# A one-core decoder layer in fp32r: the order of instructions made with a timeline simulation in place of the plain machine model

## The chip, the cores and the metric

The kernel runs on one core of a Trainium2 chip. The metric is the device time of one launch in microseconds; lower is better. Engines are named as in the profile: PE is TensorE, DVE is VectorE, ACT is ScalarE, POOL is GpSimd and SP is SyncE, which issues most of the DMAs. L394 is line 394 of the kernel.

## The reference, cut to what matters

One layer on 1024 tokens of width 1024, all in float32: a norm, a token mixer of two parallel branches (RG-LRU and HGRN2), an output projection with a residual, a second norm, a squared-ReLU MLP with a residual, and a last norm.

```python
h = rms_norm(x, norm_mix)
xa, ga, q, f, v, g, m_a, m_b = split(h @ w_in)            # 8 projections of 1024 x 1024
y_a = rg_lru(conv4(xa), ...) * gelu(ga)                   # a scan over the tokens, channel by channel
o   = hgrn2_chunkwise(silu(q), k(f), log_f(f), v)         # 8 heads, chunks of 32 tokens, a 128x128 state per head
y_b = rms_norm(o, hg_norm) * silu(g)                      # norm over the 128 channels of a head
x   = x + (sigmoid(m_a) * y_a + sigmoid(m_b) * y_b) @ w_out
h   = rms_norm(x, norm_mlp)
x   = x + square(relu(h @ w_up)) @ w_down                 # 1024 -> 4096 -> 1024
out = rms_norm(x, norm_final)
```

## The kernel before

**Matrix products.** Each float32 operand is split into a high and a low fp32r part: ACT casts the high part (L76), DVE subtracts it from the source for the low part (L77). One product is then three matmuls of PE, high by high (L115), high by low (L116) and low by high (L117). Weights of the mixer come as tiles of 128 x 1024 (raw, L84), and each is split into wH and wL (`split_w`), two tiles ahead.

**Mixer.** The 1024 tokens are two chunks (c = 0, 1) of 512, and the 1024 channels are 4 pairs (p) of two 128-channel heads. A pair takes nine weight tiles' worth of projections in the order v, xa, q, f, rg, g, mb, ga, ma. From xa come the convolution (L301 to L311) and RG-LRU with its scan (L337 to L354); pr and pi are its two gate products. From q, f and v comes HGRN2: on each head the decay inside a chunk of tokens is built up in levels. PE multiplies small blocks of queries and keys into score banks (`sc1`, `sc2`, `sc8`, all L394, then `sc32` L479 and `sc64` L497); between the levels DVE multiplies queries and keys by further decays (L384, among them q, qb, kk and seg) and picks out the scores (L404, L438). Then, head after head (06 and 07, 16 and 17 are the two heads of the last pair), PE transposes the keys (`pk`, L525), ACT copies them (`kT`, L527), PE makes the state's increments (`pkv`, L531), DVE advances the state (`sn`, L545, L547), and PE makes the outputs (`po` of the pair, L538 and L541). ACT squares them for the norm of the head (`on`, L551) and copies them (L554), DVE adds the epsilon (`hssq`, L555), POOL raises to the power of -1/2 (`hrs`, L557) and DVE multiplies (on by hrs, L384). The gates follow (L565 to L596): PE transposes on (`poT`, L586), DVE multiplies it into `g2` (L587), and the sum `sma` (L595, L596) is split into y0H, y0L (chunk 0) or y1H, y1L, the operands of the output projection.

**Output projection and norms.** After the four pairs of chunk 0 comes `out_proj` (banks po000 to po013, weight tiles 68 to 75; the operand of the last pair meets wH71 and wH75), with the first norm of chunk 1 in between: the normed rows xn are transposed by PE (`xT_x`, L145) and split into hT. After chunk 1, the second output projection is mixed with the second norm: rows x2a and x2s, `norm_rows` (rstd_h, L137; xn_h, L139), transposes `xT_h` (L704), copies `braw` (L705), and sums and differences of quarters (`combos`, L666 to L669).

**MLP.** Both products are made with a seven-step scheme on quarters (X, Y and Z banks; `uX`, `uY`, `uZ` for up, `dX`, `dY`, `dZ` for down). Operands of the first are h2B11, h2T4 and the like, of the weights wA, ws1 to ws4. Up runs over 16 quads of 7 steps, and its squared results (b, then u, split once more) are kept in DRAM (L837, L897) but for the last two. Down runs over 8 blocks of two quads, in two halves of 7 steps each, and adds into acc (L963). `finish` (L924 to L934) is the last norm and the store.

**What sets the order.** The code above is the program's order; the order on every engine is made by the library's scheduler when the program is built. It places instructions one after another, taking among those that are ready by its view of when each engine is free and by priority. A few hints bind it: `keep_in_program_order` on the first norm of chunk 0, `tc.high_priority` of 400 around the weight splits, 300 around RG-LRU, 160 around the weights of one late quad. The pools limit it too: a tile is reused only after its last reader, with bufs tiles of a tag (4 of raw, 6 of w; of the PSUM banks 4 of pj for products, 2 of sc, and 2 of hg for the transposes and states). The engines then run their queues in that order, with semaphores for the dependences.

## Time and profile before

| | before |
|---|---|
| time, median of 3 runs (lowest to highest) | 1631.38 us (1631.27 to 1631.52) |
| span of the profiled execution, first to last instruction | 1628.7 us |
| mean granted clock of TensorE | 0.996 |
| busy: PE, DVE, ACT, POOL | 1584.9, 1212.7, 764.4, 65.8 us |
| moved by DMA | 246.51 MB, 151 GB/s |

The times are of whole launches; the profiled execution is known by its span, and the 2.7 us between it and the median lie outside the first and the last instruction. PE busy is the time in which at least one matmul is in the array; what it leaves of the span is idle time of PE. The stages follow each other in the trace: first norm to about 28 us, chunk 0 of the mixer to about 449, output projection to about 497, chunk 1 to about 927, its output projection and the second norm to about 1012, MLP up to about 1306, MLP down to about 1619, tail.

### The profile page before, as it was taken

Reading aid. Unit: us, or ns where it says so; the run is one execution under the profiler, and the core shown is the slowest. Engines: PE = TensorE matmul, PEld = TensorE weight load, DVE = VectorE, ACT = ScalarE, POOL = GpSimd, SP = SyncE. Lnnn points to the kernel's source line nnn. Section 1 sums busy time; section 2 is a strip of 40 time slices with the busy share of each in tenths; the row PEclk is TensorE's granted clock in tenths of the full one; section 3 lists DMA queues with packets and bytes.
Section 4 is the critical chain, followed back from the end, with each engine's and each line's share of the span. In section 5 each row is a group of like instructions: output and inputs, shape, how many; then the busy total and the mean of one; then the engine's idle time right before and its main releaser. Section 6 shows DMA issues by size and latency. Waiting matters only on the chain.

```text
span 1628.7 us, 23177 instructions
## 1 busy us (share of the span) xinstructions
PE 1584.9 (97%) x9240; PEld 1303.1 (80%) x9240; DVE 1212.7 (74%) x1751; ACT 764.4 (47%) x1186; POOL 65.8 (4%) x99
## 2 busy tenths in 40 slices
PE   7999999999999999999999997999999999999998
PEld 6788788788788788787787876888878878888886
DVE  5975956848764865848759688977777888888876
ACT  4643545435442544436434566766776731222113
POOL 0010100100100000100100100000000000000000
PEclk9999999999999999999999998999999999999999
DMA  6212212122243222222122352666656575666652
GB/s 237 91 66 91 91 66 103 66 91 91 80 167 136 86 78 90 80 78 101 69 91 91 117 207 104 250 246 250 235 233 248 222 269 228 251 244 251 254 203 104
DMA packets 57996, 246.51 MB, mean 151 GB/s; under 512 B 6688, under 2 KB 6816, under 8 KB 47136
## 3 DMA queue, kind: packets, MB, share of 16 engines
q1 hardware_dynamic: 56304, 239.27, 39.3%
q10 hardware_dynamic: 1584, 5.77, 1.0%
q8 instruction: 72, 1.18, 0.3%
q14 instruction: 36, 0.29, 0.1%
HBM read 185.24 MB, written 59.77 MB: 150 GB/s over the span
## 4 chain that ended last, share of the span: by engine, by line
PE 80%; DVE 16%; DMA 2%; issue 1%; ACT 1%; POOL 0%; DVEq 0%; POOLq 0%; SPq 0%; ACTq 0%
PE dX L115 3%; PE uX L115 3%; PE uX L117 3%; PE uX L116 3%; PE dX L116 3%; PE dX L117 3%; DVE wL L77 2%; PE pj_ga L117 2%; PE pj_ga L116 2%; PE pj_ga L115 2%; PE pj_f L117 2%; PE pv L115 2%; PE pv L117 2%; PE pv L116 2%; PE pj_ma L117 2%; PE pj_ma L116 2%
## 5 line engine op out<-in xcount | busy, mean ns | idle before, releaser
L77 DVE TENSOR_TENSOR wL<-raw,wH 128x1024 fp32r<-128x1024 f32 x160 | 194.3, 1214 | 150.0 <-ACT wH L76 145.8
L76 ACT CAST wH<-raw 128x1024 fp32r<-128x1024 f32 x160 | 167.9, 1050 | 168.1 <-issue 66.4
L963 DVE TENSOR_TENSOR acc<-acc,dX 128x512 f32<-128x512 f32 x128 | 85.2, 684 | 31.2 <-PE dX L117 30.1
L76 ACT CAST wA<-q 128x512 fp32r<-128x512 f32 x32 | 19.8, 621 | 129.6 <-PE dX L117 103.7
L963 DVE TENSOR_TENSOR acc<-acc,dY 128x512 f32<-128x512 f32 x64 | 43.6, 686 | 17.3 <-PE dY L117 15.7
L345 DVE RECIPROCAL rr<-rr 128x512 f32<-128x512 f32 x16 | 53.5, 3347 | 0.0
L823 ACT ACTIVATE b<-b 128x512 f32<-128x512 f32 x48 | 30.2, 631 | 38.6 <-DVE b L822 38.5
L115 PE MATMUL pv<-wH,hT0H 128*128 128x256 f32 x128 | 37.4, 292 | 0.0
L116 PE MATMUL pv<-wL,hT0H 128*128 128x256 f32 x128 | 37.0, 289 | 0.0
L117 PE MATMUL pv<-wH,hT0L 128*128 128x256 f32 x128 | 37.0, 289 | 0.0
L115 PE MATMUL pv<-wH,hT1H 128*128 128x256 f32 x128 | 36.5, 285 | 0.0
L117 PE MATMUL pv<-wH,hT1L 128*128 128x256 f32 x128 | 36.2, 283 | 0.0
L116 PE MATMUL pv<-wL,hT1H 128*128 128x256 f32 x128 | 36.2, 283 | 0.0
L311 DVE SCALAR_TENSOR_TENSOR xc<-xp,pvt,xc 128x512 f32<-128x512 f32 x48 | 33.1, 746 | 0.0
L551 ACT ACTIVATE on<-po 128x128 f32<-128x128 f32 x64 | 17.0, 278 | 33.5 <-PE po L541 33.2
L570 ACT ACTIVATE smb<-pj_mb 128x512 f32<-128x512 f32 x16 | 9.6, 598 | 45.3 <-PE pj_mb L117 45.2
L824 ACT ACTIVATE b<-b 128x512 f32<-128x512 f32 x48 | 30.1, 630 | 1.1
L77 DVE TENSOR_TENSOR wA<-q,wA 128x512 fp32r<-128x512 f32 x32 | 22.0, 687 | 9.9 <-ACT wA L76 9.7
L444 POOL TENSOR_SCALAR seg<-seg 128x128 f32<-128x128 f32 (+1 forms) x16 | 14.5, 905 | 361.1 <-DVE seg L384 361.1
L565 ACT ACTIVATE g<-pj_g 128x512 f32<-128x512 f32 x16 | 9.6, 600 | 37.2 <-PE pj_g L117 37.2
L384 DVE TENSOR_TENSOR seg<-seg 128x128 f32<-128x128 f32 (+2 forms) x96 | 26.7, 307 | 0.2
L117 PE MATMUL pj_ga<-hT1H,wL 128*128 128x512 f32 x64 | 26.5, 414 | 0.0
(1854 smaller groups left out, 5261.5 us busy)
## 6 DMA issues: line engine op xcount, KB each, us to landing
raw<-wts_in SPq DMA_DIRECT2D x160, 512.0 KB, 3.4
q<-mlp_in SPq DMA_DIRECT2D x64, 512.0 KB, 3.9
x<-x_in SPq DMA_DIRECT2D x8, 512.0 KB, 6.1
acc<-x ACTq DMA_DIRECT2D x8, 512.0 KB, 6.1
y_out<-acc SPq DMA_DIRECT2D x16, 256.0 KB, 2.1
xs<-x_in SPq DMA_DIRECT2D x8, 256.0 KB, 3.5
x<-xs SPq DMA_DIRECT2D x8, 256.0 KB, 2.3
x2s<-x_in SPq DMA_DIRECT2D x4, 512.0 KB, 4.7
```

The costliest lines, as they stand in the source:

```text
L76: keep(A.copy(h, src))
L77: keep(V.tensor_tensor(out=lo, in0=src, in1=h.bitcast(F32), op=ALU.subtract))
L115: PE.matmul(o, ah, bh, start=first, stop=False, **how)
L116: PE.matmul(o, ah, bl, start=False, stop=False, **how)
L117: PE.matmul(o, al, bh, start=False, stop=last, **how)
L311: V.scalar_tensor_tensor(xc[:, s, :], xp[:, j : j + T], pvt[:, PV_CW + 8 * j + u : PV_CW + 8 * j + u + 1], xc[:, s, :], op0=ALU.mult, op1= ...
L345: V.reciprocal(rec, rec)
L384: mul = lambda o, a, b: V.tensor_tensor(out=o, in0=a, in1=b, op=ALU.mult)
L551: A.activation(on[:, 4 * s + n, :], po[:, n * P : (n + 1) * P], AF.Square, accum_out=ssq[:, 4 * s + n : 4 * s + n + 1])
L823: A.activation(b[:, at, :], b[:, at, :], AF.Relu, scale=-1.0 if at == 2 else 1.0)
L824: A.activation(b[:, at, :], b[:, at, :], AF.Square)
L963: V.tensor_tensor(out=dst, in0=dst, in1=banks[bk, pr], op=op)
```

## The change

One argument is passed where the program is built: the scheduler takes its times from the library's timeline simulation of the program instead of its plain machine model. No instruction is added, removed or resized: 8104 matmuls and transposes, 1753 instructions of DVE, 1103 of ACT, 104 of POOL and 393 of SP are in both programs. Their order differs: on PE 6505 instructions stand at another place (half of all by 20 places or more, at most 172), on DVE 1513 (half by 4 or more, at most 34), on ACT 852, on SP 122 and on POOL 23. The semaphore waits and which buffer of a pool a tile gets follow from the order; PE has 1019 waits where it had 879.

```diff
     o = nc.dram_tensor("y_out", (S, D), F32, kind="ExternalOutput").ap()
-    with tile.TileContext(nc) as tc:
+    with tile.TileContext(nc, schedule_with_timeline_sim=True) as tc:
         trunk(tc, *args, o)
     r = _run(nc, [arrays], core_ids=[0])
```

## The prediction

> **What bounds the kernel now.** I read the page's totals first, then the busy time by stage, then PE's waits, then the timeline of the places where a wait could appear. Totals and chain:
>
> ```profile
> PE 1584.9 (97%) x9240; PEld 1303.1 (80%) x9240; DVE 1212.7 (74%) x1751; ACT 764.4 (47%) x1186; POOL 65.8 (4%) x99
> PE 80%; DVE 16%; DMA 2%; issue 1%; ACT 1%; POOL 0%; DVEq 0%; POOLq 0%; SPq 0%; ACTq 0%
> ```
>
> TensorE is busy for 1584.9 of the span of 1628.7 us. The set of instructions is the same after the change, so what it can win is the remainder, 43.8 us, and everything else it does can only add idle time. So the question is where those 43.8 us lie. The view of busy time by stretch gives it, cut at the kernel's stages (mixer chunk 0, its output projection, mixer chunk 1, its output projection with the second norm, MLP up, the change to MLP down, MLP down, tail); the columns behind the stretch are its length and each engine's busy time, then the granted clock:
>
> ```profile
> core 0: us, PE busy (x) PEld busy (x) DVE busy (x) ACT busy (x) POOL busy (x), PEclk, DMA share, GB/s
> 0.00:100.00 100.00, 86.73 (x642) 72.08 (x643) 77.59 (x143) 50.99 (x73) 10.05 (x25) 1.00 0.40 144
> 100.00:427.00 327.00, 322.45 (x2299) 270.46 (x2298) 230.14 (x346) 151.44 (x249) 24.23 (x34) 1.00 0.25 85
> 427.00:500.00 73.00, 72.82 (x366) 60.86 (x365) 39.67 (x51) 29.22 (x54) 3.31 (x4) 1.00 0.38 135
> 500.00:927.00 427.00, 421.39 (x2992) 351.88 (x2992) 294.80 (x436) 196.04 (x325) 21.69 (x28) 1.00 0.25 87
> 927.00:1020.00 93.00, 81.72 (x370) 65.02 (x369) 78.87 (x111) 61.34 (x99) 6.48 (x8) 0.94 0.46 166
> 1020.00:1300.00 280.00, 280.00 (x1200) 224.44 (x1199) 226.78 (x282) 194.67 (x274) 0.00 (x0) 1.00 0.62 242
> 1300.00:1340.00 40.00, 39.29 (x168) 30.92 (x167) 35.85 (x49) 14.82 (x21) 0.00 (x0) 1.00 0.77 287
> 1340.00:1600.00 260.00, 259.90 (x1129) 211.47 (x1128) 206.75 (x292) 55.86 (x67) 0.00 (x0) 1.00 0.57 225
> ```
>
> PE's idle time is 13.3 us in the first 100 us, 4.6 and 5.6 in the mixer chunks, 0.2 in the first output projection, 11.3 around the second norm, 0.7 at the change to MLP down, none in the rest of the MLP, and the remaining 8 in the tail. The view of waits says what PE waited for (total, times, longest):
>
> ```profile
> PE xT_h L704 <- DVE rstd_h L137: 6.2, 2, 5.5
> PE sc L394 <- DVE qb L384: 5.0, 8, 0.6
> PE sc L394 <- DVE q L384: 4.0, 8, 0.5
> PE xT_h L704 <- DVE xn_h L139: 1.8, 3, 1.1
> PE uX L115 <- ACT ws30H L76: 1.7, 1, 1.7
> PE uZ L115 <- ACT braw L705: 1.1, 1, 1.1
> ```
>
> The mixer's idle time is one habit repeated: in each of the 8 pairs PE comes to two of the HGRN score blocks (sc, L394) half a microsecond before DVE's product is there.
>
> **The change part by part.** Comparing the two instruction orders, the arithmetic is untouched and the places move on every engine. Six places matter; the sum is made against the profiled span, which lies 2.7 us under the median of the timed runs (1631.38), a gap I keep.
>
> *Mixer, 8 pairs.* The new order puts each pair's HGRN blocks later in PE's queue, behind more of the following projections. Counted in 512-column projection matmuls, the first score block moves by 3, the second (sc2) by 39, sc8 by 57, sc32 by 70, sc64 by 88, the state blocks pk and po by about 100, and the transposes poT (L586) by 89. A projection matmul passes every 0.23 us (rows 993.16 and 993.40 below), so PE comes 0.7 us later to the first block and 9 us later to the second, against waits of 0.5 and 0.6. Between sc2 and sc8 lie 31 matmuls now (7 us) where 13 lay. Both waits go: 5.0 + 4.0 = 9.0 us. Gain -9.0, bounded by 0 (DVE falls behind too) and -10.2 (all idle time of both stretches).
>
> *First output projection.* A pair's delayed chain hides under the next pair's projections; the last pair of a chunk has none. In the new order PE's queue ends pk07, pkv07, po07, poT030, poT031, eight transposes of the next norm, and then the first out_proj product that needs this pair's y0 (wH71), with nothing else between. What this chain lasts can be read off the profile of before, where it ran under the ga projection (timeline; start, length, engine):
>
> ```profile
> 427.30 0.60 PE L525 MATMUL pk<-ident,kk 128*128 128x128 f32 x4
> 427.50 0.28 ACT L551 ACTIVATE on<-po 128x128 f32<-128x128 f32 x1 [3.04 <-PE po L541]
> 428.52 0.60 ACT L527 COPY kT<-pk 128x512 f32<-128x512 f32 x1
> 431.75 0.39 PE L541 MATMUL po<-sn,qf 128*128 128x128 f32 x2
> 433.60 0.17 DVE L555 TENSOR_SCALAR hssq<-hssq 128x8 f32<-128x8 f32 x1
> 433.85 1.64 POOL L557 TENSOR_TENSOR hrs<-hssq,mhalf 128x8 f32<-128x8 f32 x1 [13.48 <-DVE hssq L555]
> 435.53 1.23 DVE L384 TENSOR_TENSOR on<-on,hrs 128x1024 f32<-128x1024 f32 x1 [1.76 <-POOL hrs L557]
> 448.57 1.03 PE L586 MATMUL poT<-ident,on 128*128 128x128 f32 x8
> 449.33 0.74 DVE L587 SCALAR_TENSOR_TENSOR g<-poT,pvt,g 128x512 f32<-128x512 f32 x1
> 451.79 0.68 DVE L596 TENSOR_TENSOR sma<-sma,g 128x512 f32<-128x512 f32 x1
> 452.50 0.62 ACT L76 CAST y0H<-sma 128x512 fp32r<-128x512 f32 x1 [2.38 <-DVE sma L596]
> ```
>
> The transposed keys kT are ready at 429.12, 1.3 us after pk's four matmuls had passed (ACT does four Squares of po06 first, as it does in the new order). The state steps sn (L545, L547) between pkv07 and po07 cost about 0.6. From po07's last matmul (431.75 + 0.39) to the end of the product on (435.53 + 1.23) it is 4.6 us: Squares, hssq, POOL's 1.64, and the product. From poT to y0H it is 0.76 + 0.74 + 0.68 + 0.62 = 2.8, of which the 16 transposes cover about 1.8, so 1.0 is left. Sum 1.3 + 0.6 + 4.6 + 1.0 = 7.5 against 0.2 idle in this stretch before: +7.3. PE takes its matmuls in the order of its queue in this trace, so nothing behind poT can fill the gap. Lower bound: 4.6, the part with no cover at all; upper: 9.1, the whole chain less the matmuls in it.
>
> *Second output projection.* The same queue end, but 15 projection matmuls stand between pk17 and pkv17, so the 1.3 goes: 0.6 + 4.6 + 1.0 = 6.2. The second norm's transposes stand later than before, and DVE catches up while PE is idle, so the short waits of xT_h (1.8 for xn_h, and 6.2 - 5.5 = 0.7 for rstd_h) go: -2.5. Net +3.7, between +2 and +6.
>
> *Second norm into MLP up.* Here DVE is what PE waits for. The new DVE order places the low half of the operand h2B11, which uX's second matmul needs, behind a norm product, a 128x512 split of a weight, one of a combination, one of the normed rows and a sum. By 1.23 for the first and 0.69 for each of the others (row below), that is 4.0 us later. It gives back the waits further on for ws30H and braw, 1.7 + 1.1 = 2.8 if all. Net +2, between 0 and +4.
>
> *MLP up to MLP down.* DVE is busy 35.85 of 40 us there. The new order lets four 128x512 weight splits go ahead of the last quads' combinations that down's first products need:
>
> ```profile
> L77 DVE TENSOR_TENSOR wA<-q,wA 128x512 fp32r<-128x512 f32 x32 | 22.0, 687 | 9.9 <-ACT wA L76 9.7
> ```
>
> 4 x 0.69 = 2.7 us later against a stretch with 0.7 idle: +2, between 0 and +2.7. Start, tail and the rest of the MLP: nothing, since PE is full there (280.00 of 280) or waits for the same loads in the same order; +-1.
>
> *Clock.* A gap of PE has a second price in this trace. Its last matmul before the 5.5 us wait ended at 979.0:
>
> ```profile
> 980.50:981.00 0.50, 0.00 (x0) 0.00 (x0) 0.50 (x2) 0.47 (x2) 0.00 (x0) 1.00 1.03 426
> 981.00:981.50 0.50, 0.00 (x0) 0.00 (x0) 0.50 (x2) 0.50 (x2) 0.00 (x0) 0.50 0.28 107
> 984.53 1.94 PE L704 MATMUL xT_h<-ident,xn_h 128*128 128x128 f32 x8 [5.54 <-DVE rstd_h L137]
> 990.18 0.63 PE L115 MATMUL uX<-h2B11H,wA 128*128 128x512 f32 x1
> 990.61 0.63 PE L116 MATMUL uX<-h2B11L,wA 128*128 128x512 f32 x1
> 991.00:991.50 0.50, 0.50 (x3) 0.42 (x2) 0.50 (x2) 0.00 (x0) 0.00 (x0) 0.76 0.21 82
> 993.16 0.39 PE L116 MATMUL uX<-h2B11L,wA 128*128 128x512 f32 x1
> 993.40 0.39 PE L117 MATMUL uX<-h2B11H,wA 128*128 128x512 f32 x1
> ```
>
> The granted clock went to 0.50 at 981.0, after 2.0 us of idleness, and came back at about 991.25, 6.7 us after PE's restart; meanwhile 512-column matmuls passed every 0.43 us, not 0.23, and eight transposes took 1.94, not 1.03. The two new gaps of 4.6 us should do the same: 16 transposes take 3.6, 0.6 more than the 2.8 + 0.2 that y0H takes anyhow, and the 3.1 us left at half clock do the work of 1.6, so 2.1 us a gap at most, 0 if the clock stays; I take 1.5 each, +3.0. [...]
>
> **Sum:** -9.0 + 7.3 + 3.7 + 2 + 2 + 3.0 = +9.0 us; 1631.4 + 9.0 = 1640.4, call it 1640. The distances from the terms to their bounds, added as squares (down 1.2, 2.7, 1.7, 2, 2, 3, 1; up 9, 1.8, 2.3, 2, 0.7, 1.2, 1), give -5.5 and +9.9: the forecast's own range is 1635 to 1650.
>
> **The rivals.** *A, faster.* Place: the second norm. Because PE stands still for 6 us earlier in that stretch, DVE arrives there without a backlog, and the wait of 5.5 us for rstd_h and its half clock (about 3: 0.9 for each of two groups of transposes and 0.2 for each of some six matmuls) go. Then -9.0 + 7.3 + 3.7 - 8.5 + 2 + 1 = -3.5, some 1628, and 1624 if the change to MLP down costs nothing and the clock holds. It decides if PE's idle time between the last out_proj matmul and uX falls below 2 us. For it: DVE is the later engine there. Against: the rstd that PE waits for is that of the last rows, which cannot start before out_proj's last matmul. Chance 0.2.
>
> *B, slower still.* Place: DVE's queue in the mixer. Its steps for sc8, sc32, po and poT now wait for PE blocks 13 to 24 us later, and in its queue behind each stand splits of weights (wL, L77, 1.21 us each) that PE needs soon. If one split per pair comes late by its own length, that is 8 x 1.2 = 10 us, and 9.0 + 10 = +19, some 1650. For it: DVE is strictly in its order, and each wait blocks all behind. Against: DVE is busy only 70% of these stretches (230.14 of 327), and PE's new order gives each chain step 3 to 7 us. It decides from an idle time of PE above 10 us in the two mixer stretches together. Chance 0.2.
>
> *C, no net effect.* The waits only change places: the 9.0 us of the pairs reappear at the chunk ends and nowhere else, and the seams of the MLP are served as before: 1631. That the change does nothing is excluded by the new order itself. Chance 0.1.
>
> **How the numbers follow.** The forecast has 0.5. About 0.2% (3.3 us) is what a measurement of this kernel can tell from no change: below 1628.1 is faster, above 1634.6 slower. Nearly all of the forecast and all of B are slower, A is mostly faster, C and the edges of both are the same: slower 0.65, faster 0.20, same 0.15. The range takes in A's middle and B: 1626 to 1654.
>
> **What would show it.** In the profile after: no more sc <- q and sc <- qb lines among PE's waits, and 100:427 and 500:927 nearly full. New lines for poT <- on of about 4.6 us, twice, near 450 and 925, with POOL hrs and DVE on right before, each followed by a granted clock of 0.5. uX later by some 2 us after the last out_proj matmul. A wait of 2 us or so near 1310. The forecast is wrong if poT has no wait, or if PE's waits for wL fill the mixer.

## The result, and the profile after

| | before | after |
|---|---|---|
| median (lowest to highest) | 1631.33 us (1630.6 to 1631.52, 4 runs) | 1655.86 us (1654.82 to 1658.14, 4 runs) |
| ratio, 95% interval | | 1.0153 [1.014, 1.0165] |
| span of the profiled execution | 1628.7 us | 1654.7 us |

The changed kernel is slower by 24.5 us. The forecast was slower by 9, with 1654 as the far end of its range; the time lies outside. The page of after, totals and chain:

```profile
PE 1587.9 (96%) x9240; PEld 1310.6 (79%) x9240; DVE 1205.1 (73%) x1751; ACT 757.0 (46%) x1186; POOL 96.8 (6%) x99
PE 90%; DVE 6%; DMA 2%; ACT 1%; issue 1%; POOL 0%; DVEq 0%; ACTq 0%; POOLq 0%
```

The same matmuls keep PE busy 3.0 us longer (1587.9 for 1584.9), and the span holds 66.8 us of idle PE instead of 43.8. Busy time by stretch, cut at the same places of the program as in the prediction (length; busy time of PE, PEld, DVE, ACT, POOL; granted clock; DMA share; GB/s):

```profile
0.00:100.00 100.00, 88.53 (x559) 74.53 (x559) 73.98 (x134) 49.79 (x70) 11.34 (x21) 1.00 0.41 149
100.00:427.00 327.00, 324.25 (x2357) 273.04 (x2356) 230.18 (x348) 151.91 (x253) 38.68 (x34) 1.00 0.25 86
427.00:510.00 83.00, 75.78 (x438) 63.92 (x437) 42.45 (x59) 28.14 (x55) 6.76 (x8) 0.96 0.36 127
510.00:940.00 430.00, 427.15 (x2995) 358.56 (x2995) 300.37 (x440) 200.62 (x325) 32.30 (x29) 1.00 0.27 95
940.00:1045.00 105.00, 83.90 (x386) 67.73 (x386) 83.59 (x119) 64.40 (x109) 7.76 (x7) 0.89 0.35 127
1045.00:1325.00 280.00, 276.88 (x1185) 220.94 (x1183) 224.72 (x282) 191.85 (x275) 0.00 (x0) 1.00 0.63 246
1325.00:1366.00 41.00, 31.51 (x117) 24.40 (x118) 25.40 (x36) 6.84 (x8) 0.00 (x0) 0.88 0.44 176
```

Length less PE's busy time, here and in the same table of before, gives the account:

| stretch | idle before | idle after | change | predicted |
|---|---|---|---|---|
| start and mixer (first, second, fourth row) | 23.4 | 17.1 | -6.4 | -9.0 |
| first output projection | 0.2 | 7.2 | +7.0 | +7.3 |
| second output projection and second norm | 11.3 | 21.1 | +9.8 | +3.7 + 2 |
| end of MLP up, change to MLP down | 0.7 | 12.6 | +11.9 | +2 |
| rest of MLP down and tail | 8.2 | 8.8 | +0.7 | 0 |
| PE's busy time (forecast for half clock) | | | +3.0 | +3.0 |
| sum | | | +26.0 | +9.0 |

The sum is that of the spans, 26.0. PE's waits in the changed kernel (total, times, longest), without the one of the start for the first normed rows (10.4 us in all, 10.1 before):

```profile
PE xT_h L704 <- ACT braw L705: 10.0, 1, 10.0
PE poT L586 <- DVE on L384: 8.9, 2, 4.5
PE dY L115 <- DVE acc L963: 7.2, 1, 7.2
PE po L541 <- DVE sn L547: 4.9, 7, 0.7
PE xT_h L704 <- DVE xn_h L139: 4.7, 1, 4.7
PE dZ L116 <- DVE wA1230L L77: 2.3, 1, 2.3
```

No sc line is left, as forecast, but seven short waits for the state step sn stand in its place, six of them (4.1 us) in the mixer's stretches and one at the second output projection. The two waits of poT are there with the size forecast (4.5). The waits of 10.0, 7.2 and 4.7 were not forecast in this size. The timeline of the first seam shows the forecast chain:

```profile
458.24 1.16 PE L531 MATMUL pkv<-v,kT 128*128 128x128 f32 x8 [1.27 <-ACT kT L527]
462.70 1.64 POOL L557 TENSOR_TENSOR hrs<-hssq,mhalf 128x8 f32<-128x8 f32 x1 [31.28 <-DVE hssq L555]
464.37 1.23 DVE L384 TENSOR_TENSOR on<-on,hrs 128x1024 f32<-128x1024 f32 x1 [1.82 <-POOL hrs L557]
465.65 1.97 PE L586 MATMUL poT<-ident,on 128*128 128x128 f32 x8 [4.49 <-DVE on L384]
469.77 0.65 PE L115 MATMUL po<-wH,y0H 128*128 128x512 f32 x1
```

A wait of 1.27 for kT, 4.49 for the product on by hrs, transposes at half speed (1.97 for eight, 1.03 in before), and out_proj 4.1 us after poT's start.

### The profile page after: what moved, and what is told of

The parts are those of the page before. It is cut to its first block, busy times and chain, and to the rows that moved or that the text cites. A ratio compares the mean times of both kernels' runs of the same rounds, so it can differ in the third digit from the quotient of the medians.

```text
span 1654.7 us, 23189 instructions
## 1 busy us (share of the span) xinstructions
PE 1587.9 (96%) x9240; PEld 1310.6 (79%) x9240; DVE 1205.1 (73%) x1751; ACT 757.0 (46%) x1186; POOL 96.8 (6%) x99
## 4 chain that ended last, share of the span: by engine, by line
PE 90%; DVE 6%; DMA 2%; ACT 1%; issue 1%; POOL 0%; DVEq 0%; ACTq 0%; POOLq 0%
PE uX L115 3%; PE uX L116 3%; PE dX L115 3%; PE uX L117 3%; PE dX L116 3%; PE dX L117 3%; PE pj_xa L115 2%; PE pj_ga L115 2%; PE pj_ga L117 2%; PE pj_ma L117 2%; PE pj_mb L117 2%; PE pj_ma L115 2%; PE pv L116 2%; PE pv L115 2%; PE pv L117 2%; PE pj_f L116 2%
## 5 line engine op out<-in xcount | busy, mean ns | idle before, releaser
L963 DVE TENSOR_TENSOR acc<-acc,dX 128x512 f32<-128x512 f32 x128 | 85.6, 683 | 40.8 <-PE dX L117 40.6
L963 DVE TENSOR_TENSOR acc<-acc,dY 128x512 f32<-128x512 f32 x64 | 42.9, 682 | 32.0 <-PE dY L117 22.4
L444 POOL TENSOR_SCALAR seg<-seg 128x128 f32<-128x128 f32 (+1 forms) x16 | 29.2, 1825 | 257.7 <-DVE seg L384 257.7
L466 POOL TENSOR_SCALAR scT<-dd 32x256 f32<-32x256 f32 x32 | 23.8, 745 | 123.5 <-DVE dd L438 122.0
L438 DVE COPY_PREDICATED dd<-mu,sc 128x192 f32<-128x192 uint8 (+2 forms) x48 | 15.5, 323 | 18.0 <-PE sc L394 17.5
L576 ACT ACTIVATE gel<-pj_ga 128x512 f32<-128x512 f32 x16 | 9.7, 604 | 38.6 <-PE pj_ga L117 38.6
L115 PE MATMUL po<-wH,y0H 128*128 128x512 f32 x64 | 25.5, 402 | 1.2 <-DVE xs L613 1.2
L557 POOL TENSOR_TENSOR hrs<-hssq,mhalf 128x8 f32<-128x8 f32 x8 | 13.2, 1645 | 222.0 <-DVE hssq L555 222.0
```

The source lines that it names most:

```text
L115: PE.matmul(o, ah, bh, start=first, stop=False, **how)
L444: G.tensor_scalar(after[:, :, 2], t4[:, :, 3], 1.0, 0.0, op0=ALU.mult, op1=ALU.add)
L466: G.tensor_scalar(scT[32 * b : 32 * b + 32, :, 32 * b : 32 * b + 32], dd[32 * b : 32 * b + 32, :, :], 1.0, 0.0, op0=ALU.mult, op1=ALU.add,)
L963: V.tensor_tensor(out=dst, in0=dst, in1=banks[bk, pr], op=op)
```

## The experiments

Most kernels below are the changed kernel in which one stretch of the program takes the order of before. For that, a table holds the instructions of the stretch, by their number in the traced program, in the order that before has on each engine, and a function chains them; all that is not in the table stays with the timeline scheduler. The table moves the line numbers of these kernels by 24 to 37 against those above (L704 is L728 or L732, L963 is L987 or L991). Each run below was timed beside the kernel before, whose median there was 1630.85 to 1632.46; the changed kernel was timed once, beside 1631.33. So a difference to the changed kernel is good to some 1.5 us, and the ratio to before is the safer number.

```diff
+ORDERS = (
+    "3107-3130 3133-3156 3159-3182 3185-3208 3218-3241 ...",   # PE
+    "3274 3282 3217 3247 3300 3277 ...",                       # DVE
+    ...
+)
+def pin(tc, nc, orders):
+    seen = {}
+    for i in nc.cur_bb.bb.instructions:
+        seen[i.name] = i
+    for words in orders:
+        ...
+                if last is not None:
+                    tc.add_manual_dep(i, last.name,
+                        mybir.DependencyInfo(mybir.DependencyClass.NoSync, mybir.DependencyReason.DATA), reason="pin")
+                last = i
...
+    pin(tc, nc, ORDERS)     # at the end of trunk
```

Three points stand for lines left out, and the remarks behind # are added here, as in the tables below. NoSync edges fix the order on one engine and add no semaphore.

### The three stretches, one at a time and together

> The changed kernel, in which every engine takes the instructions traced for pair 03, the first output projection and the first norm of chunk 1 in their order of before; everything else is left to the timeline scheduler. Theory (the late chain of the last pair leaves PE idle, and idle time of PE is never given back): the two waits around poT030 (4.5 us on DVE's product, 1.3 us on kT07) go, PE's idle time between 427 and 510 falls from 7.2 to under 1 us, the granted clock stays 1.00 there, and with 1 to 2 us of half clock the time falls by 7 to 9 us against the changed kernel, to 1647 to 1649. Rival (the idle time only changes place, because DVE or the DMAs are behind): the same microseconds appear as waits in the first pair of chunk 1 and the time falls by less than 3.

Measured: 1649.47 us, 1.0113 [1.0095, 1.013] of before; 6.4 us less than the changed kernel. Both waits at poT030 are gone, with no new wait beyond the half microseconds of sc in pair 03. The theory's mechanism holds; the gain lies just under its 7 to 9.

> The changed kernel with the order of before for what is traced from pair 13 to the first three quads of MLP up (second output projection, second norm); the rest is left to the timeline scheduler. Theory (order inside this stage costs 9.8 us of idle PE and 1 to 2 us of half clock): the waits xT_h on braw (10.0), xT_h on xn_h (4.7) and poT on the product of hrs (4.4) go, the wait of 5.5 for rstd_h comes back, and the time falls by 9 to 12 us, to 1644 to 1647. Rival (the second norm is late since DVE arrives with a backlog from the mixer): the wait before uX stays above 10 us and the time falls by less than 5.

Measured: 1647.77 us, 1.0101 [1.0083, 1.0118]; 8.1 us less. PE's waits in the stretch are those of before again (5.6 for rstd_h, 1.7 for ws30H), and a new wait of 4.1 us for b stands later, in MLP up. The theory's mechanism holds, with less gain than it said.

> The changed kernel with the order of before for what is traced from quad 13 of MLP up to the second block of MLP down (weight splits, last combinations, loads of acc and of u); the rest is left to the timeline scheduler. Theory (the 7.2 us wait of dY for acc, the waits for wA1230, and the half clock behind them are the order's work): PE's idle time from 1300 to 1366 falls from 12.6 to about 1 us and the time by 10 to 13 us, to 1643 to 1646. Rival (the loads are late because the DMA queues are full whatever their order): the wait for acc stays above 4 us and the time falls by less than 6.

Measured: 1650.48 us, 1.0127 [1.0101, 1.0152]; 5.4 us less. That is half of the theory's gain and within the rival's, but the rival's sign, a wait for acc above 4 us, is absent: that wait did vanish, and the borders of the stretch made three others:

```profile
PE uX L142 <- ACT e L846: 3.2, 2, 2.7
PE dX L142 <- DMA u0n<-u0n: 2.1, 1, 2.1
PE dY L142 <- DMA u2t<-u2t: 2.0, 1, 2.0
```

So it was run again without the far border:

> The changed kernel with the order of before for everything traced from quad 13 of MLP up to the end, so without the far border that gave the earlier run of this stretch new waits for u0n and u2t. Theory (the order from the last quads into MLP down costs 11.9 us of idle PE and about 1 us of half clock): the time falls by 9 to 13 us against the changed kernel, to 1643 to 1647; what is left of new waits lies at the near border, in MLP up. Rival (most of the loss is a lag that the order before quad 13 carries in): less than 6 us.

Measured: 1645.46 us, 1.009 [1.0077, 1.0104]; 10.4 us less. The loads' waits are gone, uX on e (3.1) at the near border stays. This is the loss that the forecast took for 2 us.

> All three stretches in their order of before together; only the mixer's pairs 00 to 02 and 10 to 12, the MLP between the stretches and the tail keep the order of the timeline scheduler. Theory (the three losses add up and the mixer's gain of some 6 us is real): 1625 to 1628, faster than the kernel before by 3 to 6 us. Rival (the mixer's gain was only the seams' loss deferred): 1631 to 1634, no faster than before.

Measured: 1634.92 us, 1.0023 [1.0013, 1.0032], nearest to the rival; the waits at the borders of the last stretch (3.5, 2.3 and 2.0 us) are in it. Without the far border, and with everything from pair 13 on in its order of before:

> The timeline scheduler's order for the mixer's pairs 00 to 02 and 10 to 12 alone: all that is traced in pair 03, the first output projection and the first norm of chunk 1, and everything from pair 13 to the end stands in its order of before. The run with three stretches of before left 7 us of new waits at the borders of the last stretch (a copy of MLP up, two loads of u); here that stretch has no far border. Theory (the mixer's new order is a true gain, 4 to 6 us of PE's idle time in the six pairs, and all losses lie elsewhere): 1625 to 1628, faster than before by 3 to 6 us. Rival (the mixer's new waits for the state copies sn eat the gain): within 2 us of before.

Measured: 1622.67 us against 1632.46 for before in the same runs, ratio 0.9946 [0.9934, 0.9959]. With a span of 1620.9 us it is the fastest kernel of all, 33 us faster than the changed one, and better than its theory said. Its stretches, to be read against those of before:

```profile
0.00:100.00 100.00, 89.91 (x557) 76.52 (x558) 74.04 (x134) 50.03 (x70) 11.37 (x21) 1.00 0.41 149
100.00:427.00 327.00, 323.52 (x2411) 272.13 (x2410) 232.47 (x356) 152.58 (x262) 38.13 (x38) 1.00 0.24 85
500.00:927.00 427.00, 423.46 (x2994) 355.33 (x2994) 300.74 (x446) 198.96 (x330) 29.93 (x29) 1.00 0.26 91
927.00:1020.00 93.00, 82.30 (x367) 65.34 (x366) 79.49 (x110) 61.65 (x98) 5.33 (x8) 0.94 0.44 158
```

Idle time in the start and the mixer is 10.1 + 3.5 + 3.5 = 17.1 us, 6.3 less than before, and 10.7 around the second norm where before has 11.3. The span is 7.8 us under that of before. The three stretches undone one at a time gave back 6.4 + 8.1 + 10.4 = 24.9 us of the 33; the other 8 are close in size to the waits that two of their borders made (4.1 for b, 3.1 for e), which this kernel does not have. The mixer's gain is real and the losses lie in the three stretches; what is left of the sc waits here (1.2 and 1.0) is that of pairs 03 and 13.

### How the loss at the second norm is made

The timeline of the changed kernel there:

```profile
992.46 1.28 DVE L139 SCALAR_TENSOR_TENSOR xn_h<-x2s,rstd_h,gain 128x1024 f32<-128x1024 f32 x1
994.86 1.28 DVE L139 SCALAR_TENSOR_TENSOR xn_h<-x2s,rstd_h,gain 128x1024 f32<-128x1024 f32 x1
996.05 1.22 DVE L77 TENSOR_TENSOR wA121L<-q,wA121H 128x1024 fp32r<-128x1024 f32 x1
997.19 1.22 DVE L77 TENSOR_TENSOR ws10L<-s,ws10H 128x1024 fp32r<-128x1024 f32 x1
998.32 0.68 DVE L77 TENSOR_TENSOR h2T4L<-braw,h2T4H 128x512 fp32r<-128x512 f32 x1
999.04 1.07 ACT L705 COPY braw<-xT_h 128x512 f32<-128x512 f32 x2 [3.85 <-DVE h2T4L L77]
999.68 1.97 PE L704 MATMUL xT_h<-ident,xn_h 128*128 128x128 f32 x8 [9.99 <-ACT braw L705]
```

PE's next transposes need a PSUM bank that ACT's copy into braw empties. The copy needs a buffer of braw (two of this tag) whose last reader is the split h2T4L of an earlier tile of rows, and DVE does that split behind a norm product and two weight splits. The order on DVE thus holds PE through a buffer. The 10.0 us are not all of this kind. PE stands idle from 989.7, and the rows that it transposes next are at the earliest those of the product at 992.46, which ends at 993.74: for the first 4 us an operand is late as well, and the last 5.9 are the buffer's alone.

> The changed kernel with one edge more: on DVE the low half h2T4L of the second tile of rows goes ahead of the weight splits wA121L and ws10L, instead of behind them. Theory (the 10.0 us wait of xT_h is a chain: PE's next transposes need ACT's copy into braw, the copy needs the buffer that h2T4L reads, and h2T4L stands behind these two splits of 1.22 us each): the wait shrinks by 2.4 us to about 7.6 and the time by 2 to 3 us. Rival (the wait is set by rstd_h and xn_h, whatever stands there): no change beyond 1 us.

```diff
+ORDERS = (
+    "8473 8862 8898",     # DVE: h2T4L, wA121L, ws10L
+)
```

Measured: the wait of xT_h on braw is 7.7 us, and the time 1653.38, 1.0131 [1.0117, 1.0145], 2.5 us less than the changed kernel. The intervals of the two kernels touch, so it is the wait, shorter by 2.3 where the theory said 2.4, that shows the chain.

> The changed kernel with DVE alone in its order of before for what is traced from pair 13 to the first three quads of MLP up; PE, ACT, POOL and SP are left to the timeline scheduler. Theory (DVE's order makes the loss at the second norm, PE's order the 4.4 us before poT130): the waits xT_h on braw (10.0) and xn_h (4.7) shrink to the 5.5 us that before has, and the time falls by 5 to 8 us against the changed kernel, to 1648 to 1651. Rival (PE's and ACT's order carry it): less than 3 us.

Measured: 1665.33 us, 1.0205 [1.0191, 1.0219], 9.5 us slower than the changed kernel; neither statement foresaw that. With DVE in one order and PE in another, PE waits for weights and for rows, among others:

```profile
PE po L140 <- DVE wL L101: 5.3, 3, 3.3
PE po L140 <- DVE rstd_h L161: 4.2, 1, 4.2
PE sc L418 <- DVE qb L408: 2.7, 1, 2.7
```

> The changed kernel with the order of before for what is traced from the second output projection to the first three quads of MLP up, but not for pair 13, whose late chain stays. Theory (the loss of 6.6 us at the second norm is made by the order inside it): the waits xT_h on braw (10.0) and on xn_h (4.7) become the 5.5 us for rstd_h, the 4.4 us before poT130 stay, and the time falls by 6 to 9 us, to 1647 to 1650. Rival (it is inherited: the late chain of pair 13 makes DVE late for the second norm): less than 3 us, and the wait before uX stays near 10.

Measured: 1656.52 us, 1.0156 [1.0142, 1.017], no gain. The waits did change as the theory said (xT_h on rstd_h 6.2 us in all, 5.5 the longest; none on braw), but a second kT wait of 1.3 at pair 13, a wait of 1.4 for y1H and one of 4.2 for b in MLP up came, and PE's busy time rose to 1592.0. The order of this stage is worth nothing without that of pair 13 ahead of it, and 8.1 us with it. Which part is handed down by the late chain and which is made at the new border isn't settled by these runs.

### PE's queue alone at the first seam

> The changed kernel with PE alone in its order of before for pair 03, the first output projection and the first norm of chunk 1; DVE, ACT, POOL and SP are left to the timeline scheduler. Theory (it is PE's queue that leaves the chain of the last pair without cover): the waits of 4.5 and 1.3 us around poT030 go as they did with all engines in their order of before, and the time falls by 5 to 8 us, to 1648 to 1651. Rival (the engines' orders only fit together, as the run with DVE alone showed at the second norm): new waits of PE for splits of weights or for sn take back more than half, and the time falls by less than 3.

Measured: 1657.08 us, 1.0161 [1.0147, 1.0175], no gain: the rival. The two waits at poT030 are gone, but earlier in pair 03, where PE now asks early, DVE is not ready:

```profile
PE sc L418 <- DVE qa L408: 3.9, 1, 3.9
PE xT_x L169 <- DVE hT1L L101: 2.1, 1, 2.1
```

So PE's queue carries the loss at the seam, as the prediction had it, only as long as the other engines' orders fit it.

### The loads at the change to MLP down

The timeline of the changed kernel (SPq and ACTq issue DMAs):

```profile
1339.71 0.33 SPq L897 DMA_DIRECT2D u0B<-u0B  x1
1343.82 1.80 ACTq L909 DMA_DIRECT2D acc<-x  x4
1352.28 0.69 DVE L963 TENSOR_TENSOR acc<-acc,dY 128x512 f32<-128x512 f32 x1 [8.50 <-DMA acc<-x]
1353.03 0.79 PE L115 MATMUL dY<-ws330H,u14B 128*128 128x512 f32 x1 [7.16 <-DVE acc L963]
```

The accumulators acc4 to acc7 are loaded behind the last splits of u15, and 2 to 4 us before them four loads of u went out (u0B, then u1B, u1t and u1n at 1340.13, 1340.61 and 1341.09). DVE waits 8.5 us for the first acc, and PE behind it for a PSUM bank that DVE's addition frees. In before, the acc loads went out ahead of the u loads:

```profile
1325.24 1.78 ACTq L909 DMA_DIRECT2D acc<-x  x4
1329.07 0.32 SPq L897 DMA_DIRECT2D u0B<-u0B  x1
```

and DVE waited 1.6 us in all for acc.

> The changed kernel with the four loads acc4 to acc7 issued by SP ahead of the u loads of the second block (u0B, u1B, u1t, u1n), instead of by ACT behind them; all else is left to the timeline scheduler. Theory (the 7.2 us wait of dY on acc is a transfer: 3.5 MB of u were put into the DMA queues 3 us before the acc loads, which then took 8.5 us): acc4 lands some 4 us after its issue, the wait shrinks to 0 to 3 us and the time by 4 to 7 us, less what the later u loads cost (up to 2 us). Rival (the loads are late because u15's last splits are late on DVE, so that the order of the transfers changes little): the wait stays above 5 us and the time falls by less than 2.

```diff
-        nc.scalar.dma_start(x2[t], x2d[t])
+        (nc.scalar if t < 4 else nc.sync).dma_start(x2[t], x2d[t])
...
+ORDERS = (
+    "11277 11279 11281 11283 11545 11553 11557 11559",     # SP: acc4 to acc7, then the u loads
+)
```

Measured: the wait of dY for acc shrinks from 7.2 to 2.0 us, the time to 1650.93, 1.0111 [1.0096, 1.0127], 4.9 us less than the changed kernel. An earlier issue is not the reason: SP issued these acc loads at 1346.28 for ACT's 1343.82, in a trace that stands 2.6 us later there (the clock falls at 1329.52 for 1326.88), so at the same point of the stage, and DVE's first addition still came sooner (1349.62 for 1352.28). What changed is that the u loads now follow, from 1348.12 on. The wait was the order of the transfers. No run took the other half of the 10.4 us apart; candidates are dZ's waits on wA1230 (2.3 and 0.9), that for u15t (1.1), and the half clock behind these gaps.

### What the mixer's gain needs

> The kernel before, under its plain scheduler, with one edit: the projection g and its sigmoid are traced ahead of HGRN2 instead of behind it. The plain scheduler then puts 1 projection matmul more ahead of a pair's first score block (0.2 us), 5 more ahead of the second (1.1 us), 9 to 12 ahead of the later ones, and leaves poT and both output projections where they were. Theory (the mixer's gain is nothing but PE coming half a microsecond later to the second score block, and the 9 us and more of the timeline scheduler are not needed): the wait of sc on qb (5.0 us in all) goes, that on q shrinks from 4.0 to about 2.4, and the time falls by 4 to 7 us, to 1625 to 1628. Rival (the chain on DVE is the limit, so that the wait moves on to sc8 or sc32): within 2 us of before.

```diff
-            on = hgrn(c, p, q1, f, kk, v)
-            gates(c, p, h, on, ys)
+            g2 = gate_g(c, p)
+            on = hgrn(c, p, q1, f, kk, v)
+            gates(c, p, h, on, ys, g2)
```

The new `gate_g`, not printed here, holds what were the first lines of `gates`: the projection g, its sigmoid and their product.

```profile
PE sc L394 <- DVE qb L384: 3.7, 8, 0.5
PE sc L394 <- DVE qa L384: 3.1, 8, 0.4
PE sc L394 <- DVE q L384: 2.2, 8, 0.3
```

Measured: 1629.92 us, 0.9994 [0.9985, 1.0003], the rival. The 9.0 us of waits are 9.0 us again, spread over three blocks of a pair instead of two. Moving the blocks by one or two microseconds moved the wait on to the next block, so the chain through DVE is the limit when they follow each other this closely. That leaves the wider spacing, of which the 31 matmuls between sc2 and sc8 are a part, as what the gain rests on; no run took that spacing alone.

## Why the prediction was wrong, step by step

**The mixer** (-9.0 predicted, -6.4 measured in this kernel). The sc waits went, as its step said. What it left out are new waits: po on sn, 0.7 us in each of six pairs (4.1 us), and pj_xa on the copy of v (1.4 us in all). In one of these pairs pkv of the second head starts at 238.03 with only matmuls of po itself behind it; the state advances in two steps on DVE (L545 at 239.12, L547 at 240.46), a weight split of 1.22 us stands between them in its queue, and PE waits from 240.17 to 240.85. The prediction priced this wait only for the last pair of a chunk. Other short waits and gaps went as well, so the net is 6.4 and not 3.5.

**The first output projection** (+7.3 predicted, +7.0 measured). Right in mechanism and in its two large pieces: 1.27 for kT (1.3), 4.49 for on (4.6). The sum is nearer than its pieces by chance: the 0.6 for sn did not come, the 1.0 behind poT was 0.3, and a wait of 1.2 for the residual rows xs, which no term had, made up for them. Undoing the stretch gives back 6.4.

**The second output projection and the second norm** (+5.7 predicted, +9.8 measured; 8.1 given back when both are undone). The 4.4 before poT130 is right. The step that failed is the price of DVE's queue in the second norm: it added the lengths of the splits ahead of h2B11L (4.0 us), set the shortened later waits against them, and let DVE catch up so that the short waits for xn_h and rstd_h would go (-2.5). The wait for xn_h rose from 1.8 to 4.7 instead. And it missed that PE would be held by a buffer: the transposes ahead of uX wait for a copy that waits for a split that waits in DVE's queue. That wait is 10.0 us where before has 5.5 for rstd_h, its last 5.9 the buffer's alone. It also priced this stage and the seam ahead of it as independent, and the run that undid the norm alone gained nothing.

**The change to MLP down** (+2 predicted, +11.9 measured; 10.4 given back). This is the largest miss. The step counted four weight splits on DVE and no DMA; of the rest of the MLP the prediction said that the loads come in the same order. At this change they did not. The acc loads stand in ACT's queue behind the last splits of u15, the u loads in SP's queue, and what came first before (acc) came second now. The order of the two in time decides who waits: 7.2 us at PE, of which 5.2 went when SP issued the acc loads first.

**The clock** (+3.0 predicted, +3.0 measured as PE's busy time). Each gap of 4.4 us or more behind the first matmul had half clock in it and behind it, two of them ahead of the output projections as forecast. The edges of the low stretch at the first output projection and of one at the change to MLP down:

```profile
463.00:463.50 0.50, 0.00 (x0) 0.00 (x0) 0.00 (x0) 0.00 (x0) 0.50 (x1) 0.80 0.00 0
470.00:470.50 0.50, 0.50 (x4) 0.41 (x4) 0.50 (x2) 0.50 (x2) 0.00 (x0) 0.87 0.00 0
1350.50:1351.00 0.50, 0.00 (x0) 0.00 (x0) 0.00 (x0) 0.00 (x0) 0.00 (x0) 0.77 1.15 483
1357.50:1358.00 0.50, 0.50 (x4) 0.42 (x3) 0.34 (x1) 0.00 (x0) 0.00 (x0) 0.91 0.00 0
```

The windows that hold no edge read 1.00 or 0.50; with these as the only values, the shares in the half microseconds place the falls at 463.3 and 1350.8 and the rises at 470.1 and 1357.6: these two low stretches last 6.8 us, and that of before (981.0 to 991.25) lasted 10.25. Read in the same way from windows of a quarter microsecond, the changed kernel has five ahead of its tail, from 463.30, 944.58, 985.54, 1326.88 and 1350.77, of 6.83, 6.83, 17.07, 3.41 and 6.83 us. In this trace all five are whole multiples of 3.41, and the falls fit one grid of 3.4133 us (from the first to the others are 141, 153, 253 and 260 steps). What PE did ahead of a fall was not the same each time: the clock fell 2.1 us after PE's last matmul at 461.2, and at 1326.88 it fell 0.6 us after PE had resumed from a gap of only 2.3 us.

That predicted and measured agree here is chance. The forecast counted two falls, and there were five. PE was busy at half clock for 20.7 us, in before for 6.3; at a matmul every 0.43 us instead of 0.23, the 14.4 us more would cost some 6.7 (an estimate from the spacing of the changed kernel's dY matmuls at 1354.04 and 1354.47 and of its dX matmuls at 1343.20 and 1343.43). Since PE's busy time rose by only 3.0, some 4 us of it must have gone elsewhere; where isn't settled by these runs.

**The rivals.** A needed a shorter wait at the second norm; it became longer. C put the waits that reappear at the chunk ends and nowhere else; the largest came in the MLP. B named DVE's order in the mixer as the place of a loss of 10 us; its time (1650) came near, but its place did not: the mixer stretches have 5.6 us of idle PE. The loss beyond the forecast lies at the stage borders of the second norm and the MLP.

## What to carry to other kernels

When a scheduler reorders everything, cost the borders between stages by following each wait through to its end: an operand, then the buffer or bank that the next instruction needs, then the transfers that stand in other queues. Orders on different engines fit together as a set, so undo or graft a stage on all of its engines at once, with borders where all engines have the same work behind them: grafting one engine alone gave nothing or lost 9.5 us where the whole stage gave back 6 to 8, and the second norm on all engines, with its border behind a late pair 13, gave nothing either. And a schedule that loses as a whole may hold a stage that wins: the mixer's new order with the old borders is 0.5% faster than before.

## What the hardware showed that was not expected

One POOL instruction, a copy of 128x128 operands between two parts of seg (L444), takes 1.33 us in the order of before and 3.41 in the new one (means of 8), while the power on 8 columns (hrs, L557) kept its 1.64. In the kernel that projects g first (z4_gfirst) it takes 0.43 in the row below. What DVE does beside it differs. The new order:

```profile
182.20 3.40 POOL L444 TENSOR_SCALAR seg<-seg 128x128 f32<-128x128 f32 x1 [4.50 <-DVE seg L384]
182.37 1.21 DVE L77 TENSOR_TENSOR wL<-raw,wH 128x1024 fp32r<-128x1024 f32 x1
183.50 1.21 DVE L384 TENSOR_TENSOR qa<-q,f 128x1024 f32<-128x1024 f32 x1
184.64 0.68 DVE L384 TENSOR_TENSOR seg<-seg 128x128 f32<-128x128 f32 x2
```

The order of before:

```profile
188.27 1.23 DVE L384 TENSOR_TENSOR qa<-q,f 128x1024 f32<-128x1024 f32 x1
188.46 1.33 POOL L444 TENSOR_SCALAR seg<-seg 128x128 f32<-128x128 f32 x1 [2.99 <-DVE seg L384]
```

z4_gfirst:

```profile
188.16 0.70 DVE L566 TENSOR_TENSOR g<-g,pj_g 128x512 f32<-128x512 f32 x1
188.35 0.43 POOL L444 TENSOR_SCALAR seg<-seg 128x128 f32<-128x128 f32 x1 [2.54 <-DVE seg L384]
```

In the new order POOL's copy lasts beyond the four DVE instructions of the rows under it, and ends 0.28 us after the last of them (185.32); in the order of before it ends 0.29 us after the end of the product qa beside it (189.50). In z4_gfirst it ends at 188.78, and DVE's product beside it only at 188.86. So the same copy took between 0.43 and 3.41 us in three orders. Which property of the DVE instructions beside it makes the difference isn't shown: they differ in length, in number and in their operands, and no run changed one of these alone. None of the long waits above names this instruction.
